# FFN input products of a two-layer diffusion step: two of the four weight sums of each block formed by transfers that add, on GpSimd's queue

## The chip, the cores and the metric

The kernel runs on one core of one Trainium2 chip. The metric is the device time of one execution in microseconds (us). The profile is one execution, recorded by the hardware profiler; instructions are put down to PE (TensorE's matmuls), PEld (its weight loads), DVE (VectorE), ACT (ScalarE), POOL (GpSimd) and SP (SyncE, which issues most transfers). A name with q behind it (SPq, POOLq) is an engine's instruction queue.

## The reference

One step of a trunk of two layers, over 512 latent and 128 context tokens (640 columns together), 1024 features, all in fp32. Each layer is an attention mixer and then a gated FFN with 2816 inner features; only the FFN matters here:

```python
def swiglu(h, w_in, w_out):
    gate, up = jnp.split(h @ w_in, 2, axis=-1)
    return (jax.nn.silu(gate) * up) @ w_out
...
        xp = xp + g2_p * swiglu(hp, w_ffn_in[l], w_ffn_out[l])
        xs = xs + g2_s * swiglu(hs, w_ffn_in[l], w_ffn_out[l])
```

## The kernel before

**Blocks.** The 2816 gate features and the 2816 up features are handled as 22 blocks of 128 (`FB` = 22). For block `fb` the weights are two tiles of 128 x 1024 fp32, `wg` (gate) and `wu` (up); columns 0 to 511 of each belong to the first 512 input features, the rest to the second 512. Every fp32 matmul is done as three: weights are split into a high part (a copy that rounds, on ACT) and a low part (the difference, on DVE), and so is the data.

**Seven products.** Blocks 0 and 1 are computed plainly (16 products of three matmuls per half of the columns). From block 2 (`FEW`) to block 21 a Strassen-Winograd scheme takes the 2 x 2 product of (gate, up) by (first, second inputs) with seven products of 12 matmuls, 320 columns each. It needs four weight operands: X is `wu` itself, W is the second half of `wg`, and Y and Z hold the four sums. With g0, g1 the halves of `wg` and u0, u1 those of `wu`: tile `s13` (Y) = [g0 + g1, u0 + g0], tile `s24` (Z) = [u0 + g0 + g1, u0 + g0 + g1 + u1]. `Weights.sums` forms the four sums on DVE, 512 columns each. `hi` and `lo` split X, Y and Z (1024 columns each), `hi_w` and `lo_w` split W (512 columns). In the profile's names, `s` stands for both `s13` and `s24`, and `wX`, `wY`, `wZ`, `wW` for the split operands.

**The loop.** `for fb in range(FEW, FB)` (L1468) issues PE's products of block `fb` and beside them prepares block `fb` + 1: `n.sums()`, then hi and lo of X, Y, Z and W. The result of block `fb` - 1 is finished there too: the gate's SiLU on ACT, the product `sg` on DVE, and its high and low parts `hd`, which SP stores to DRAM (`sp`). `step` brings the next layer's modulation weights `wm` (512 KB a block) and multiplies them on DVE into `junk`. `fetch_u` and `fetch_g` load the tiles `wu` and `wg` of block `fb` + 2 on SP's queue: `wu` into the pool `rawp` (3 buffers, shared with `wm`), `wg` into tag `wr` (2 buffers).

**The opening.** Before the loop, `ffn` computes blocks 0 and 1 and the first product of blocks 2 and 3 (`ahead`), while `ModS.make` and `add_up` form the seven data operands D, N, C, E and the two quarters of h (names `h01D`, `h01q` and so on in layer 0, `h11...` in layer 1). The unsplit data lies in spare tiles, `h0132a` (tag `cb`), `h0132d` (two, tag `wr`) and `h0132e` (tag `w4`); so the first `wg` tiles of the loop wait until `add_up` has read the `wr` tiles. The weights of block 1, `wgu_10` and `wgu_11`, come through two raw tiles of tag `ws`.

**Order.** Each engine runs its own list in order. The lists are made when the program is built: the framework's scheduler places instructions by the order of the code, by when it expects operands and buffers to be ready, and by `issue_after` hints; `Line` chains most of the loop's DVE work, and its ACT work, in the order in which it is written. A transfer waits on its queue until its buffer is free, and holds what is behind it in that queue.

Of the kernel before, what the change touches and what calls it, by code (L numbers as in the profile page):

```python
# [11 lines left out]
F32 = mybir.dt.float32  # L12
F32R = mybir.dt.float32r
AF = mybir.ActivationFunctionType
ALU = mybir.AluOpType
# [35 lines left out]
def body(ctx, tc, xT, vecs, crow, wm0, wm0g, wm1, wA, wNV, wNA, wMK, wMV, wOA, wGQ, wGK, wGV, wOC,  # L51
# [53 lines left out]
    def f(ap):  # L105
        return ap.bitcast(F32)
# [55 lines left out]
    def load(src, n, name):  # L162
        raw = rawp.tile([P, 1024], F32, tag="raw", name=name)
        nc.sync.dma_start(raw[:, :n], src)
        return raw[:, :n]
# [94 lines left out]
    class ModS:  # L260


        def __init__(self, name, x, gsl, ml, sh, pools):
            pool, keep_ = pools

            a = keep_.tile([P, 2 * D], F32, tag="cb", bufs=1, name=name + "32a")
            d = [pool.tile([P, 1024], F32, tag="wr", bufs=2, name=f"{name}32d{i}") for i in range(2)]
            d += [pool.tile([P, 1024], F32, tag="w4", bufs=2, name=f"{name}32e{i}") for i in range(2)]
            room = [t[:, j * HT:j * HT + HT] for t, n in zip([a] + d, (6, 3, 3, 3, 1)) for j in range(n)]
            self.left, self.right = room[:KT], room[KT:]  # L270
            self.name, self.x, self.gsl, self.ml, self.sh = name, x, gsl, ml, sh
            self.act = {}
            self.q = [[ring.tile([P, T], F32R, tag=("hh", "hl")[i], name=f"{name}q{k}{i}") for k in range(KT)] for i in range(2)]
            self.sums = {c: [pool.tile([P, T], F32R, tag="sums", bufs=16, name=f"{name}{c}{k}") for k in range(4)]
                         for c in "DCNE"}
# [927 lines left out]
    def ffn_open(l):  # L1203

        ph = ExitStack()
        fk = ph.enter_context(tc.tile_pool(name=f"fk{l}", bufs=1, reuse_waits="tile"))
        dr = ph.enter_context(tc.tile_pool(name=f"dr{l}", bufs=1, space=bass.MemoryType.DRAM))
        hd = [[fk.tile([P, T], F32R, name=f"hd{l}_{i}{c}") for c in "hl"] for i in range(1)]
        fs = ExitStack()
        fp = fs.enter_context(tc.tile_pool(name=f"fp{l}", bufs=1, reuse_waits="tile"))  # L1210
        w = []

        def pre():
            for i in range(2):
                w.append(unit(wFI[l, 0, i], 1024, f"wgu{l}_{i}", "vg"[i], pool=fp))
            w.append(unit(wFI[l, FEW, 1], 1024, f"wX{l}_{FEW}", pool=fp))
        return ph, fk, dr, hd, fs, fp, w, pre

    def scale_final(x, c, k):
# [3 lines left out]
    def ffn(l, x, pend, hm, nxt, side, opened):  # L1223
# [95 lines left out]

        def fetch_u(fb):  # L1320
            if fb < FB:
                raws[fb] = [load(wFI[l, fb, 1], 1024, f"wu{l}_{fb}r")]

        def fetch_g(fb):
            if fb == FEW:
                raws[fb].append(load(wFI[l, fb, 0], 1024, f"wg{l}_{fb}r"))
            elif fb < FB:
                rg = fp.tile([P, 1024], F32, tag="wr", bufs=2, name=f"wg{l}_{fb}r")
                nc.sync.dma_start(rg, wFI[l, fb, 0])
                raws[fb].append(rg)  # L1330

        class Weights:

            def __init__(self, fb):
                self.fb = fb
                self.u, self.g = raws[fb]
                self.X = wX[fb - FEW] if fb < FEW + AHEAD else None

            def sums(self):
                ru, rg = self.u, self.g  # L1340
                s13 = fp.tile([P, 1024], F32, tag="ws", bufs=2, name=f"s13{l}_{self.fb}")
                dve(V.tensor_tensor, s13[:, :512], rg[:, :512], rg[:, 512:], ALU.add)
                dve(V.tensor_tensor, s13[:, 512:], ru[:, :512], rg[:, :512], ALU.add)
                s24 = fp.tile([P, 1024], F32, tag="ws", bufs=2, name=f"s24{l}_{self.fb}")
                dve(V.tensor_tensor, s24[:, :512], s13[:, 512:], rg[:, 512:], ALU.add)
                dve(V.tensor_tensor, s24[:, 512:], s24[:, :512], ru[:, 512:], ALU.add)
                self.s = {"X": ru, "Y": s13, "Z": s24}
                self.t = {c: wtile(f"w{c}{l}_{self.fb}") for c in "XYZ" if c != "X" or self.X is None}
# [10 lines left out]
            def hi_w(self):  # L1359
                t = fp.tile([P, 2, 512], F32R, tag="w4", bufs=2, name=f"wW{l}_{self.fb}")  # L1360
                self.W = two(t)
                act(S.activation, self.W[0], self.g[:, 512:], AF.Copy)

            def lo_w(self):
                dve(V.tensor_tensor, self.W[1], self.g[:, 512:], f(self.W[0]), ALU.subtract)

        done = hm.done
        eight(0, w0, 0, range(3))
# [2 lines left out]
        wX = [w0[2]]  # L1371
        ahead(FEW, wX[0])
        wX += [unit(wFI[l, FEW + i, 1], 1024, f"wX{l}_{FEW + i}", behind=done) for i in range(1, AHEAD)]
        w1 = [unit(wFI[l, 1, i], 1024, f"wgu{l}_1{i}", behind=done, raw=fp.tile([P, 1024], F32, tag="ws", bufs=2, name=f"wgu{l}_1{i}r"))
              for i in range(2)]
        fetch_u(FEW)
        fetch_g(FEW)
# [90 lines left out]
        for fb in range(FEW, FB):  # L1468

            first = fb < FEW + AHEAD  # L1470
            n = Weights(fb + 1) if fb < FB - 1 else None
            b5 = bank(f"fd{l}_{fb}")
            up = tmp(f"up{l}_{fb}")
            sg = lead if paired and PAIR_OF.get(fb, (0, 1))[1] == 0 else tmp(f"sg{l}_{fb}")
            both = paired and job and job[0] in PAIR_OF
            p5, u1, g2 = [utile(f"{c}{l}_{fb}") for c in ("p5", "u1", "g2")]
            if n:
                n.sums()
            if n and not first:
                n.hi("X")  # L1480
            if fb in early:
                g = early[fb][0]
            else:
                g, b2, p1 = bank(f"fg{l}_{fb}"), bank(f"fu{l}_{fb}", "y"), utile(f"p1{l}_{fb}")
                product(g, w.X, 0, 11, True)
                act(S.activation, p1, g[:, :HT], AF.Copy)
            if n and not first:
                n.hi("Y")
                n.lo("X")
                n.hi("Z")  # L1490
                n.lo("Y")
                fetch_u(fb + 2)
            after(PE.last, lambda: product(b5, w.Y, 0, "D", True))
            act(S.activation, p5, b5[:, :HT], AF.Copy)
            if n and not first:
                n.lo("Z")
            if job:
                jb, jg, jW, jup, jsg = job
                product(jg, jW, 0, "E", False)
                if jb in early:  # L1500
                    dve(V.tensor_tensor, jsg[:, HT:T], jup[:, HT:T], jsg[:, HT:T], ALU.mult)
                act(S.activation, jsg[:, 0:HT], jg[:, :HT], AF.Silu, scale=-1.0)
                if jb in early:
                    dve(V.tensor_tensor, jsg[:, 0:HT], early[jb][1], jsg[:, 0:HT], ALU.mult)
                else:
                    dve(V.tensor_tensor, jsg, jup, jsg, ALU.mult)
            if n and not first:
                n.hi_w()
            if both:
                split_pair(jb, jsg, 0)  # L1510
            elif job:
                dh, dl = room(), room()
                act(S.activation, dh, jsg, AF.Copy)
            product(g, w.Z, 0, "N", False)
            act(S.activation, u1, g[:, :HT], AF.Copy)
            if n:
                if first:
                    for c in "XYZ":
                        n.hi(c)
                        n.lo(c)  # L1520
                    fetch_u(fb + 2)
                    n.hi_w()
                n.lo_w()
                fetch_g(fb + 2)
            if both:
                split_pair(jb, jsg, 1)
            elif job:
                dve(V.tensor_tensor, dl, jsg, f(dh), ALU.subtract)
                spill(jb, dh, dl)
            if fb not in early:  # L1530
                product(b2, w.X, 512, 21, True)
                dve(V.tensor_tensor, up[:, 0:HT], b2[:, :HT], p1, ALU.add)
            if both:
                split_pair(jb, jsg, 2)
            step("fb", fb, dve)
            step("load", fb + 1, act)
            product(b5, w.Z, 512, 22, False)
            dve(V.tensor_tensor, up[:, HT:T], b5[:, :HT], u1, ALU.add)
            product(g, w.Y, 512, "C", False)
            dve(V.tensor_tensor, g2, g[:, :HT], p5, ALU.add)  # L1540
            act(S.activation, sg[:, HT:T], g2, AF.Silu, scale=-1.0)
            job, w = (fb, g, w.W, up, sg), n
# [728 lines left out]
```

## Time and profile before

| | |
|---|---|
| times of three runs | 1481.51, 3368.07, 1478.6 us; median 1481.51 us |
| the profiled execution | 1480.2 us; its span 1478.4 us |
| PE busy | 1440.5 us, 97% of the span |
| DVE busy | 1202.6 us, 81% |
| ACT busy | 769.9 us, 52% |
| POOL busy | 210.9 us, 14% |
| FFN of layer 0, of layer 1 (input part) | about 377 to 650 us, about 1045 to 1318 us |

The span runs from the first to the last instruction of the profile; the rest of the execution's own time, 1.8 us, lies around it. A row of the timeline gives start, duration, engine, line, operation, output<-input, shapes and count; a duration includes the instruction's pipeline, so instructions that follow each other can start a little sooner than the one before has ended. A row of the table by stage gives, for each engine, the busy time and the number of instructions in that stage, then the clock granted to TensorE, the mean busy share of the 16 DMA engines, and GB/s.

### The profile page before, as it was taken

What the parts mean: (1) busy time and instruction counts of PE and PEld (TensorE: products, weight loads), DVE (VectorE), ACT (ScalarE), POOL (GpSimd) and SP (SyncE); (2) the same over time, 40 slices, a digit from 0 to 9 for tenths busy, and PEclk for the clock granted to TensorE, in tenths of its full rate; (3) what the DMA queues carried; (4) which work ended last, traced back from release to release, by engine and by line L of the source; (5) the groups of instructions that cost most, each with busy time, mean ns of one, the idle gap of its engine ahead of it and who ended that gap; (6) DMA issues with size and microseconds to landing.
All of it is one profiled execution on the core that took longest, in us unless ns stands there. A gap on an engine that the chain in (4) does not pass through costs nothing.

```text
span 1478.4 us, 25725 instructions
## 1 busy us (share of the span) xinstructions
PE 1440.5 (97%) x9785; PEld 1391.9 (94%) x9785; DVE 1202.6 (81%) x2236; ACT 769.9 (52%) x1521; POOL 210.9 (14%) x302
## 2 busy tenths in 40 slices
PE   5999999999999999999999999999999999999997
PEld 3988888889999999999999999989999999999996
DVE  5686688876989999967997888766999999954496
ACT  5446677863754544441123666663755555542253
POOL 0326534422000000000002322212000000000000
PEclk9999999999999999999999999999999999999998
DMA  9544521015065555569863210013055555668522
GB/s 372 219 152 142 178 67 37 29 55 189 30 204 190 189 184 182 168 229 336 271 217 114 95 55 31 29 44 123 29 196 169 190 197 209 207 224 303 196 86 72
DMA packets 80651, 229.53 MB, mean 155 GB/s; under 512 B 9136, under 2 KB 14736, under 8 KB 80144
## 3 DMA queue, kind: packets, MB, share of 16 engines
q1 hardware_dynamic: 77600, 220.51, 44.4%
q0 software_dynamic: 1728, 5.33, 1.0%
q10 hardware_dynamic: 1200, 2.05, 0.4%
q8 instruction: 77, 1.26, 0.3%
q14 instruction: 46, 0.38, 0.1%
HBM read 192.97 MB, written 34.89 MB: 154 GB/s over the span
## 4 chain that ended last, share of the span: by engine, by line
PE 85%; DVE 6%; ACT 4%; DMA 2%; issue 2%; SPq 0%; POOL 0%; DVEq 0%; ACTq 0%; POOLq 0%
PE fg L63 21%; PE fd L63 10%; PE fo L63 8%; PE fu L63 6%; PE gq L63 3%; DMA mraw<-in_wm 2%; PE nk L63 2%; PE nq L63 2%; PE fo_2b L63 1%; PE fo_0b L63 1%; PE gs L63 1%; PE fo_2a L63 1%; PE fo_0a L63 1%; PE go L63 1%; PE fo_4b L63 1%
## 5 line engine op out<-in xcount | busy, mean ns | idle before, releaser
L1805 DVE SCALAR_TENSOR_TENSOR junk<-wm,cb 128x1024 bf16<-128x1024 f32 x62 | 75.7, 1221 | 5.4 <-DMA wm<-in_wm 4.7
L1248 ACT ACTIVATE sg<-g 128x320 f32<-128x320 f32 x34 | 16.0, 472 | 115.0 <-DVE g L1248 115.0
L63 PE MATMUL gq<-h10h,wgq 128*128 128x320 f32 x256 | 66.7, 318 | 0.0
L255 POOL TENSOR_SCALAR h10h<-h10t,gs,mods 128x320 fp32r<-128x320 f32 x4 | 3.6, 888 | 429.5 <-DVE h10t L249 427.8
L1248 DVE SCALAR_TENSOR_TENSOR junk<-wm,cb 128x1024 bf16<-128x1024 f32 x50 | 61.1, 1221 | 0.8
L1248 DVE TENSOR_TENSOR wY<-s,wY 128x1024 fp32r<-128x1024 f32 x40 | 48.8, 1220 | 2.2 <-ACT wY L1248 2.2
L1248 DVE TENSOR_TENSOR wZ<-s,wZ 128x1024 fp32r<-128x1024 f32 x40 | 48.8, 1220 | 0.0
L63 PEld LDWEIGHTS gq<-h10h,wgq 128*128 128x128 f32 x256 | 45.0, 188 | 0.9 <-PE gtp L67 0.2
L1248 ACT ACTIVATE wZ<-s 128x1024 fp32r<-128x1024 f32 x40 | 42.4, 1060 | 0.1
L1248 ACT ACTIVATE wY<-s 128x1024 fp32r<-128x1024 f32 x40 | 42.0, 1049 | 0.0
L63 PE MATMUL gq<-h10l,wgq 128*128 128x320 f32 x128 | 39.5, 308 | 0.0
L1987 ACT ACTIVATE gp<-gs,gb,rq 128x640 f32<-128x640 f32 (+1 forms) x40 | 31.9, 797 | 14.5 <-DVE gb L1986 14.1
L63 PE MATMUL fg<-h11E,wW 128*128 128x320 f32 x240 | 38.7, 310 | 0.0
L63 PE MATMUL fg<-h11q,wX 128*128 128x320 f32 x240 | 38.6, 309 | 0.0
L63 PE MATMUL fg<-h01q,wX 128*128 128x320 f32 x240 | 38.6, 309 | 0.0
L63 PE MATMUL fg<-h11N,wZ 128*128 128x320 f32 x240 | 38.6, 309 | 0.0
L63 PE MATMUL fg<-h01N,wZ 128*128 128x320 f32 x240 | 38.6, 309 | 0.0
L63 PE MATMUL fu<-h01q,wX 128*128 128x320 f32 x240 | 38.6, 309 | 0.0
L63 PE MATMUL fu<-h11q,wX 128*128 128x320 f32 x240 | 38.6, 309 | 0.0
L63 PE MATMUL fg<-h01E,wW 128*128 128x320 f32 x240 | 38.6, 309 | 0.0
L63 PE MATMUL fd<-h11q,wZ 128*128 128x320 f32 x240 | 38.5, 309 | 0.0
L63 PE MATMUL fd<-h01q,wZ 128*128 128x320 f32 x240 | 38.5, 309 | 0.0
(3227 smaller groups left out, 5236.5 us busy)
## 6 DMA issues: line engine op xcount, KB each, us to landing
wm<-in_wm SPq DMA_DIRECT2D x48, 512.0 KB, 4.0
mraw<-in_wm SPq DMA_DIRECT2D x8, 1024.0 KB, 15.4
mraw<-in_wm SPq DMA_DIRECT2D x16, 512.0 KB, 3.9
hr_T<-sp_T SPq DMA_DIRECT2D x21, 320.0 KB, 5.8
hr_B<-sp_B SPq DMA_DIRECT2D x18, 320.0 KB, 6.2
mrow<-in_wm0g POOLq DMA_DIRECT2D x8, 512.0 KB, 6.4
wm<-in_wm0g SPq DMA_DIRECT2D x8, 512.0 KB, 3.5
x<-in_xT SPq DMA_DIRECT2D x8, 320.0 KB, 5.4
```

The costliest lines, as they stand in the source:

```text
L63: cls.last = nc.tensor.matmul(*a, **k)
L255: G.tensor_scalar(h[:, c0:c1], t, self.gsl[:, k, 0:1], self.ml[:, self.sh + k, 0:1], ALU.mult, ALU.add)
L1248: self.last = after(self.last, lambda: op(*a, **k))
L1805: def step(kind, at, line=lambda op, *a, **k: op(*a, **k)):
L1987: weighed.append((S.activation(dst, src, AF.Exp, bias=nb, scale=rq[:, j:j + 1], accum_out=ll[:, j:j + 1]), v))
```

## The change

The two sums of `s13` are no longer instructions of DVE. The tile `wg` grows to 1536 columns, and three transfers fill it for blocks 3 to 21 (block 2 stays as it was): SP writes g0 twice into columns 0 to 1023; once that has landed, a transfer on GpSimd's queue reads g1 and u0 from DRAM and adds them to these columns in place; SP writes g1 alone into columns 1024 to 1535. `fetch_g` now stands right behind `n.sums()`, earlier in the loop. To make room, `s24` has one buffer instead of two, the spare tiles of the opening are laid out differently, and the raw tiles of block 1's weights come from the tags `w4` and `ws`.

```diff
-            d = [pool.tile([P, 1024], F32, tag="wr", bufs=2, name=f"{name}32d{i}") for i in range(2)]
-            d += [pool.tile([P, 1024], F32, tag="w4", bufs=2, name=f"{name}32e{i}") for i in range(2)]
-            room = [t[:, j * HT:j * HT + HT] for t, n in zip([a] + d, (6, 3, 3, 3, 1)) for j in range(n)]
+            d = [pool.tile([P, 1536], F32, tag="wr", bufs=2, name=f"{name}32d{i}") for i in range(2)]
+            d.append(pool.tile([P, 1024], F32, tag="w4", bufs=2, name=f"{name}32e"))
+            room = [t[:, j * HT:j * HT + HT] for t, n in zip([a] + d, (6, 4, 4, 2)) for j in range(n)]
...
+            w.extend(fp.tile([P, 1024], F32, tag=tag, bufs=n, name=f"wgu{l}_1{i}r") for i, (tag, n) in enumerate((("w4", 2), ("ws", 1))))
...
-                rg = fp.tile([P, 1024], F32, tag="wr", bufs=2, name=f"wg{l}_{fb}r")
-                nc.sync.dma_start(rg, wFI[l, fb, 0])
-                raws[fb].append(rg)
+                t = fp.tile([P, 1536], F32, tag="wr", bufs=2, name=f"wg{l}_{fb}r")
+                g, y = wFI[l, fb, 0], t[:, :1024].rearrange("p (a b) -> p a b", a=2)
+
+                def from_(at, step):
+                    return bass.AP(tensor=g.tensor, offset=g.offset + at, ap=[list(g.ap)[0], [step, 2], [1, 512]])
+                nc.sync.dma_start(y, from_(0, 0))
+                nc.gpsimd.dma_start(y, from_(512, P * 1024 - 512), accum_op=ALU.add)
+                nc.sync.dma_start(t[:, 1024:], g[:, 512:])
+                raws[fb, 0] = t
...
-                s13 = fp.tile([P, 1024], F32, tag="ws", bufs=2, name=f"s13{l}_{self.fb}")
-                dve(V.tensor_tensor, s13[:, :512], rg[:, :512], rg[:, 512:], ALU.add)
-                dve(V.tensor_tensor, s13[:, 512:], ru[:, :512], rg[:, :512], ALU.add)
-                s24 = fp.tile([P, 1024], F32, tag="ws", bufs=2, name=f"s24{l}_{self.fb}")
-                dve(V.tensor_tensor, s24[:, :512], s13[:, 512:], rg[:, 512:], ALU.add)
+                ru, s13 = self.u, self.s13
+                if s13 is None:
+                    s13 = fp.tile([P, 1024], F32, tag="w4", bufs=2, name=f"s13{l}_{self.fb}")
+                    dve(V.tensor_tensor, s13[:, :512], self.g0, self.g, ALU.add)
+                    dve(V.tensor_tensor, s13[:, 512:], ru[:, :512], self.g0, ALU.add)
+                s24 = fp.tile([P, 1024], F32, tag="ws", bufs=1, name=f"s24{l}_{self.fb}")
+                dve(V.tensor_tensor, s24[:, :512], s13[:, 512:], self.g, ALU.add)
...
             if n:
                 n.sums()
+                fetch_g(fb + 2)
...
                 n.lo_w()
-                fetch_g(fb + 2)
```

How the built lists change. On DVE in the middle of the loop, from the sums of block 9 to its Z, before (wg_9r and wu_9r are the raw tiles):

```order
L1248 TENSOR_TENSOR s_9_6007<-wg_9r 128x512
L1248 TENSOR_TENSOR s_9_6007<-wu_9r,wg_9r 128x512
L1248 TENSOR_TENSOR s_9_6010<-s_9_6007,wg_9r 128x512
L1248 TENSOR_TENSOR s_9_6010<-s_9_6010,wu_9r 128x512
L1248 TENSOR_TENSOR wX_9_6013<-wu_9r,wX_9_6013 128x1024
L1248 TENSOR_TENSOR wY_9_6014<-s_9_6007,wY_9_6014 128x1024
L1248 TENSOR_TENSOR wZ_9_6015<-s_9_6010,wZ_9_6015 128x1024
```

and now:

```order
L1249 TENSOR_TENSOR s_9_6002<-wg_9r 128x512
L1249 TENSOR_TENSOR s_9_6002<-s_9_6002,wu_9r 128x512
L1249 TENSOR_TENSOR wX_9_6005<-wu_9r,wX_9_6005 128x1024
L1249 TENSOR_TENSOR wY_9_6006<-wg_9r,wY_9_6006 128x1024
L1249 TENSOR_TENSOR wZ_9_6007<-s_9_6002,wZ_9_6007 128x1024
```

Two sums are gone, the first remaining one reads the tile that the added transfer fills, and nothing else of the block has moved. On SP, the transfers of one block in the middle of the loop, before:

```order
L1329 DMA wg_10r<-in_wFI 128x1024
L1282 DMA sp_6h<-hd_0h 128x640
L1282 DMA sp_6l<-hd_0l 128x640
L164 DMA wu_10r<-in_wFI 128x1024
L164 DMA wm_44_6108<-in_wm0g 128x1024
```

and now; the third transfer of the tile stands behind the two stores, and the adding transfer is a row of POOL's list:

```order
L1334 DMA wg_10r<-in_wFI 128x2x512
L1283 DMA sp_6h<-hd_0h 128x640
L1283 DMA sp_6l<-hd_0l 128x640
L1336 DMA wg_10r<-in_wFI 128x512
L164 DMA wu_10r<-in_wFI 128x1024
L164 DMA wm_44_6102<-in_wm0g 128x1024
```

The first transfer of the tile stands where the one of before stood: both wait for `lo_w` of block 8, the last reader of the buffer. POOL's list, which held nothing in this part of the program, gets one row for each of the blocks 3 to 21, each writing the tile wg that SP's first transfer has filled:

```order
L1335 DMA wg_9r<-in_wFI 128x2x512
L1335 DMA wg_10r<-in_wFI 128x2x512
L1335 DMA wg_11r<-in_wFI 128x2x512
```

In the opening of the FFN (layer 0; layer 1 alike), the low parts of block 1's weights and the sums of block 2 (wg_2r, wu_2r) stood on DVE among the low parts of the data's right half (L298):

```order
L298 TENSOR_TENSOR h01q_4718<-h0132d_4706,h01q_4718 128x320
L185 TENSOR_TENSOR wgu_10_4988<-wgu_10r,wgu_10_4988 128x1024
L298 TENSOR_TENSOR h01q_4719<-h0132d_4706,h01q_4719 128x320
L185 TENSOR_TENSOR wgu_11_4993<-wgu_11r,wgu_11_4993 128x1024
L298 TENSOR_TENSOR h01q_4720<-h0132d_4706,h01q_4720 128x320
L298 TENSOR_TENSOR h01q_4721<-h0132e_4707,h01q_4721 128x320
L1248 TENSOR_TENSOR s_2_5003<-wg_2r 128x512
```

Now they stand behind all of those, and behind the gate of block 0 (`sg_0`) and part of `add_up` (L310 to L313):

```order
L1307 TENSOR_TENSOR sg_0_4999<-fu_00_4852,sg_0_4999 128x320
L312 TENSOR_TENSOR h0132a<-h0132a,h0132d_4707 128x320
L313 SCALAR_TENSOR_TENSOR h0132a<-h01n_5023,h0132a 128x320
L185 TENSOR_TENSOR wgu_10_4988<-wgu_10r,wgu_10_4988 128x1024
L185 TENSOR_TENSOR wgu_11_4992<-wgu_11r,wgu_11_4992 128x1024
L1249 TENSOR_TENSOR s_2_5002<-wg_2r 128x512
```

On ACT the two high parts moved likewise, from ahead of the right half's data to right behind the table load and the SiLU of block 0:

```order
L1306 ACT_TABLE_LOAD
L1306 ACTIVATE sg_0_4999<-fg_00_4851 128x320
L184 ACTIVATE wgu_10_4988<-wgu_10r 128x1024
L184 ACTIVATE wgu_11_4992<-wgu_11r 128x1024
```

They moved behind the table load, which is a wait that they did not stand behind before. Behind the sums of block 2, `add_up` and the gates follow on DVE as before, except that the second half of block 1's gate (`sg_1`) now stands ahead of the low part of block 2's Z (`wZ_2`). Outside the two FFN input parts the lists of all engines are the same.

More of the change, by code (lines that the diff above doesn't have):

```diff
@@ L1321, in fetch_u @@
             if fb < FB:
-                raws[fb] = [load(wFI[l, fb, 1], 1024, f"wu{l}_{fb}r")]
+                raws[fb, 1] = load(wFI[l, fb, 1], 1024, f"wu{l}_{fb}r")
         def fetch_g(fb):
             if fb == FEW:
-                raws[fb].append(load(wFI[l, fb, 0], 1024, f"wg{l}_{fb}r"))
+                raws[fb, 0] = load(wFI[l, fb, 0], 1024, f"wg{l}_{fb}r")
             elif fb < FB:
-                rg = fp.tile([P, 1024], F32, tag="wr", bufs=2, name=f"wg{l}_{fb}r")
-                nc.sync.dma_start(rg, wFI[l, fb, 0])
-                raws[fb].append(rg)
+                t = fp.tile([P, 1536], F32, tag="wr", bufs=2, name=f"wg{l}_{fb}r")
[6 more added lines that the diff above has]
+                raws[fb, 0] = t
         class Weights:
@@ L1335, in __init__ @@
                 self.fb = fb
-                self.u, self.g = raws[fb]
+                self.u, g = raws[fb, 1], raws[fb, 0]
+                self.g, self.s13 = (g[:, 512:], None) if fb == FEW else (g[:, 1024:], g[:, :1024])
+                self.g0 = g[:, :512]
                 self.X = wX[fb - FEW] if fb < FEW + AHEAD else None
             def sums(self):
-                ru, rg = self.u, self.g
-                s13 = fp.tile([P, 1024], F32, tag="ws", bufs=2, name=f"s13{l}_{self.fb}")
-                dve(V.tensor_tensor, s13[:, :512], rg[:, :512], rg[:, 512:], ALU.add)
-                dve(V.tensor_tensor, s13[:, 512:], ru[:, :512], rg[:, :512], ALU.add)
-                s24 = fp.tile([P, 1024], F32, tag="ws", bufs=2, name=f"s24{l}_{self.fb}")
-                dve(V.tensor_tensor, s24[:, :512], s13[:, 512:], rg[:, 512:], ALU.add)
+                ru, s13 = self.u, self.s13
[5 more added lines that the diff above has]
+                dve(V.tensor_tensor, s24[:, :512], s13[:, 512:], self.g, ALU.add)
                 dve(V.tensor_tensor, s24[:, 512:], s24[:, :512], ru[:, 512:], ALU.add)
@@ L1361, in hi_w @@
                 self.W = two(t)
-                act(S.activation, self.W[0], self.g[:, 512:], AF.Copy)
+                act(S.activation, self.W[0], self.g, AF.Copy)
             def lo_w(self):
-                dve(V.tensor_tensor, self.W[1], self.g[:, 512:], f(self.W[0]), ALU.subtract)
+                dve(V.tensor_tensor, self.W[1], self.g, f(self.W[0]), ALU.subtract)
         done = hm.done
@@ L1373, in ffn @@
         wX += [unit(wFI[l, FEW + i, 1], 1024, f"wX{l}_{FEW + i}", behind=done) for i in range(1, AHEAD)]
-        w1 = [unit(wFI[l, 1, i], 1024, f"wgu{l}_1{i}", behind=done, raw=fp.tile([P, 1024], F32, tag="ws", bufs=2, name=f"wgu{l}_1{i}r"))
+        w1 = [unit(wFI[l, 1, i], 1024, f"wgu{l}_1{i}", behind=done, raw=w0[3 + i])
               for i in range(2)]
```

## The prediction

> **What bounds the kernel now.** I read the page's shares first, then the table by stage for the two FFN input parts, then the waits of PE, then one block on the timeline. The page:
>
> ```profile
> span 1478.4 us, 25725 instructions
> PE 1440.5 (97%) x9785; PEld 1391.9 (94%) x9785; DVE 1202.6 (81%) x2236; ACT 769.9 (52%) x1521; POOL 210.9 (14%) x302
> GB/s 372 219 152 142 178 67 37 29 55 189 30 204 190 189 184 182 168 229 336 271 217 114 95 55 31 29 44 123 29 196 169 190 197 209 207 224 303 196 86 72
> ```
>
> PE is idle for 1478.4 - 1440.5 = 37.9 us in all. That is the most that any relief of another engine can win. Where does that idleness lie? The table by stage has both FFN input parts whole, and one stretch of three blocks in each:
>
> ```profile
> 395.00:650.00 255.00, 255.00 (x1740) 254.81 (x1740) 238.30 (x361) 130.69 (x222) 0.00 (x0) 1.00 0.55 178
> 1064.00:1318.00 254.00, 254.00 (x1733) 253.81 (x1733) 236.31 (x379) 139.04 (x251) 0.00 (x0) 1.00 0.57 188
> 444.00:481.00 37.00, 37.00 (x254) 37.00 (x254) 36.08 (x53) 18.77 (x32) 0.00 (x0) 1.00 0.60 189
> 1258.00:1295.00 37.00, 37.00 (x254) 37.00 (x254) 36.56 (x62) 21.13 (x39) 0.00 (x0) 1.00 0.63 206
> ```
>
> PE is busy for all of 255 and all of 254 us there, at a granted clock of 1.00, so none of the 37.9 us is in the parts that the change touches. The waits of PE say the same from the other side; the longest ones carry the names of a norm and of the final norm, and asked for those two stretches alone, the view has no entry:
>
> ```profile
> PE n00p L63 <- DVE n00acc L215: 7.9, 1, 7.9
> PE fn1p L63 <- DVE fn1acc L215: 1.8, 1, 1.8
> ```
>
> DVE, at 36.08 of 37 us, looks like a second bound, and it is not: it keeps step, and what it makes is ready ahead of PE. One block on the timeline:
>
> ```profile
> 470.45 1.22 DVE L1248 TENSOR_TENSOR wX<-wu_8r,wX 128x1024 fp32r<-128x1024 f32 x1
> ...
> 479.84 0.68 DVE L1248 TENSOR_TENSOR s<-wg_9r 128x512 f32<-128x512 f32 x1
> 480.44 0.69 DVE L1248 TENSOR_TENSOR s<-wu_9r,wg_9r 128x512 f32<-128x512 f32 x1
> 481.16 0.69 DVE L1248 TENSOR_TENSOR s<-s,wg_9r 128x512 f32<-128x512 f32 x1
> ...
> 486.64 0.69 DVE L1248 TENSOR_TENSOR wW<-wg_9r,wW 128x512 fp32r<-128x512 f32 x1
> ...
> 491.88 0.68 DVE L1248 TENSOR_TENSOR s<-wg_10r 128x512 f32<-128x512 f32 x1
> ```
>
> ```profile
> 478.44 1.92 PE L63 MATMUL fg<-h01q,wX 128*128 128x320 f32 x12
> ...
> 490.75 1.93 PE L63 MATMUL fg<-h01q,wX 128*128 128x320 f32 x12
> ```
>
> PE takes a block every 490.75 - 478.44 = 12.31 us, DVE's sums come every 491.88 - 479.84 = 12.04 us, and block 8's X is ready at 471.67, 6.8 us before PE starts on it at 478.44.
>
> **The change part by part.** *The sums that go.* Start to start, the two of block 9 take 0.60 + 0.72 = 1.32 us. Over blocks 3 to 21 of two layers, 38 blocks, DVE loses about 38 x 1.3 = 49 us of work. To the end this is worth nothing, because PE's 12.31 us a block cover all of DVE's 12.04; were that cover gone, up to 1.3 us a block would count. It buys slack: DVE needs about 10.7 of every 12.3 us.
>
> *The wait that is added, in the steady loop.* SP's first transfer stands where the old load stood and waits for the same reader, wW of two blocks before:
>
> ```profile
> 475.31 0.33 SPq L1329 DMA_DIRECT2D wg_10r<-in_wFI  x1
> ```
>
> The old load then had 491.88 - 475.31 = 16.6 us until its first reader. Now the first transfer (about 4.2 us, the row below), and behind it the adding one, A us from issue to landing, must both land. From a block's sums to the wW that frees its buffer DVE takes 486.64 + 0.69 - 479.84 = 7.5 us, less 1.3 for the two sums that go: 6.2 us. A buffer goes round in two blocks, 24.6 us, so the loop keeps PE's pace while 4.2 + A + 6.2 is below 24.6: A up to 14 us costs nothing. Behind DVE's waiting sum stand all the low parts of that block and its gate, behind ACT's waiting high part of Y those of Z and W; on POOL nothing but the next block's transfer, with POOL busy for 0.00 us in all four stages.
>
> No row shows an adding transfer, so A is bounded by the nearest ones: plain transfers, with queue, count, size and median time to landing, and for the one tile that POOL loads, its shortest, median and longest.
>
> ```profile
> wg_10r<-in_wFI SPq DMA_DIRECT2D x2, 512.0 KB, 4.2
> mraw<-in_wm SPq DMA_DIRECT2D x8, 1024.0 KB, 15.4
> mrow<-in_wm0g POOLq DMA_DIRECT2D x8, 512.0 KB, 6.4
> ...
> DMA to landing us min/median/max: 3.9/6.4/11.8
> wg_3r<-in_wFI SPq DMA_DIRECT2D x1, 512.0 KB, 3.4
> cb<-in_crow SPq DMA_DIRECT2D x1, 1024.0 KB, 5.0
> ```
>
> From below: 3.4 us, a plain load of this size with little beside it. From above: 15.4 us, a load that moves in bytes what this one reads twice over, in the busiest part of the program. My value: POOL's shortest, 3.9, plus the destination read as well, 512 KB at the rate of the stage above (189 GB/s at a share of 0.60 is 315 GB/s at full share, so 1.7 us), is 5.6; with other transfers beside it, A = 6. That is near POOL's own median of 6.4.
>
> The Trainium skill (DMA: Bandwidth & Descriptors, section Anatomy of one DMA — SWDGE (gpsimd) path) gives a fit for plain transfers from GpSimd of 2.0 us plus the bytes at 436 GB/s, an estimate of 3.2 us here. By it, without a second read, the sum below would lose its second term and be 1481.5; the shortest row on POOL, 3.9 us, is already longer than the fit.
>
> *The opening*, where the cover is thin. Layer 0; layer 1 repeats it 668.4 us later.
>
> ```profile
> 387.69 1.22 DVE L185 TENSOR_TENSOR wgu<-wgu_10r,wgu 128x1024 fp32r<-128x1024 f32 x1
> 389.23 1.22 DVE L185 TENSOR_TENSOR wgu<-wgu_11r,wgu 128x1024 fp32r<-128x1024 f32 x1
> ...
> 398.39 0.49 DVE L313 SCALAR_TENSOR_TENSOR h0132a<-h01n,h0132a 128x320 f32<-128x320 f32 x1
> ...
> 404.81 0.50 DVE L312 TENSOR_TENSOR h0132a<-h0132a,h0132d 128x320 f32<-128x320 f32 x1
> ...
> 409.63 1.23 DVE L1248 TENSOR_TENSOR wY<-s,wY 128x1024 fp32r<-128x1024 f32 x1
> ...
> 411.50 1.24 DVE L1248 TENSOR_TENSOR wZ<-s,wZ 128x1024 fp32r<-128x1024 f32 x1
> ```
>
> ```profile
> 394.13 1.28 ACT L1305 ACT_TABLE_LOAD   x1
> 395.42 0.44 ACT L1305 ACTIVATE sg<-fg 128x320 f32<-128x320 f32 x1
> ```
>
> ```profile
> 399.07 0.60 PE L63 MATMUL fg<-h01q,wgu 128*128 128x320 f32 x3
> ...
> 413.16 1.93 PE L63 MATMUL fd<-h01D,wY 128*128 128x320 f32 x12
> 414.92 1.92 PE L63 MATMUL fg<-h01N,wZ 128*128 128x320 f32 x12
> ...
> 420.20 1.93 PE L63 MATMUL fd<-h01D,wY 128*128 128x320 f32 x12
> ```
>
> ACT's high parts of wgu now stand behind that SiLU, from about 395.8 to 397.8, and DVE's low parts behind the gate that waits for the same SiLU (ends 395.86) and two rows of `add_up`: from about 397.2 to 399.5. Block 1 begins on PE at 399.07, and its third matmul, the first to need a low part, some 0.3 us later; the low part of the first tile is there at 398.4. That just fits. But what DVE did before the SiLU it now does after it, two low parts and four sums, 2 x 1.14 + 4 x 0.6 = 4.7 us, against 398.79 - 397.2 = 1.6 us by which it is there sooner. All of DVE behind is 3.1 us late. wY_2's low part ends at 410.86 + 3.1 = 414.0, against a D product that starts at 413.16 and needs it about 0.7 us in: level. wZ_2's, 0.4 further back behind `sg_1`, ends at 412.74 + 3.5 = 416.2, needed at about 415.6: PE loses 0.65 us, my first term.
>
> ```profile
> 405.38 0.33 SPq L1329 DMA_DIRECT2D wg_3r<-in_wFI  x1
> 407.75 0.33 SPq L1795 DMA_DIRECT2D cb<-in_crow  x1
> ```
>
> The first transfer for block 3 takes the buffer that held `h0132d`, and waits for its last read, the L312 row at 404.81, now at about 408. It is issued at 408.4 and lands at about 412.8, beside the 1 MB of `cb`; the adding one lands at 412.8 + A. From then DVE needs two sums (1.2), `hd_0l` (0.7) and wY_3's low part (1.2), and PE needs that at 420.20 + 0.65 + 0.3 = 421.1. So PE waits for max(0, A - 5) us: 1.0 at A = 6, my second term.
>
> *The sum.* 2 x (0.65 + 1.0) = 3.3 us on the profiled execution's 1480.2: **1483.5 us**. That execution and the median, 1481.51, differ by 0.1%. At A = 3.4 it is 1481.5; at 15.4 the opening takes 2 x (0.65 + 10.4) = 22 us and the loop (15.4 - 14)/2 a block, 0.7 x 36 = 25: 1527.
>
> **The rivals.** *No loss at all* (wY_2 and the waits of the opening fall into slack that I misjudged by a us): 1477 to 1481. For it speaks that PE's waits have no entry there; against it, that I count the lag row by row.
>
> *The transfers become the bound, slower than before.* 16 engines are busy for 0.60 x 12.31 = 7.4 us a block, 0.63 in layer 1, 7.8. The third transfer adds 256 KB, 0.8 us at the rate above; the adding one, read twice, 3.3 us. That makes 11.5 to 11.9 of 12.31 us: inside, but with little over, and if adding costs more engine time than a second read, past it. It decides from 12.31 - 7.8 - 0.8 = 3.7 us of all engines, 2.2 times a plain transfer's 1.7. At three times, 5.0 us, a block takes 7.6 + 0.8 + 5.0 = 13.4 us: 1.1 x 38 = 42 us and the opening, 1527; at four times 1590. Against it: a slice of the page reaches 372 GB/s, so the share counts waiting as well as moving, and the 189 GB/s of a block would rise to 189 + 64 = 253 for the 768 KB written more, 296 with the second read. Late transfers would show first in `wm`, issued only 4.9 us ahead of its reader (SP's row, then DVE's), where a load of this size takes about 4.2:
>
> ```profile
> 483.74 0.33 SPq L164 DMA_DIRECT2D wm<-in_wm0g  x1
> ...
> 488.67 1.21 DVE L1248 SCALAR_TENSOR_TENSOR junk<-wm,cb 128x1024 bf16<-128x1024 f32 x1
> ```
> The Trainium skill (DMA: Bandwidth & Descriptors, section Issuing engines are not separate DMA queues) says that transfers of all issuers interleave on the same 16 engines, so POOL's queue would bring no room of its own; the shares above count as if that held.
>
> *DVE was the bound after all.* Then 49 us go: 1431. Against it stands 255.00 of 255.00 us on PE.
>
> *The change doesn't do what it says*, sums or their waits not gone from DVE's path: about 1480, as before.
>
> **How the numbers follow.** Forecast (opening loses 1 to 10 us, the loop nothing) 0.60; no loss 0.17; transfers the bound, or A over 14, 0.18; DVE the bound 0.03; no change in what DVE does 0.02. 2% of the median, about what a measurement of this kernel can tell from no change, is 30 us: 1452 to 1511. Forecast, no loss and no effect lie within, 0.79; the slower rival starts at its edge, 0.18. The range takes in the upper end of A, which is also three times a plain transfer, and leaves out the DVE rival and about half of the slow one: 1476 to 1527.
>
> **What would show it.** DVE busy at about 1154 us, PE's waits still empty in both parts but for about 1.6 us at 415 to 421 and again 668 us later, the adding transfer landing in about 6 us, DMA share at 0.8 to 0.95. Wrong would be: a PE wait for wY, wZ or `s` in block after block, PE rows further apart than 12.31 us, or an adding transfer over 14 us.

## The result, and the profile after

The changed kernel takes 1501.53 us in the median (1498.57 to 1502.7), against 1480.1 us: a ratio of **1.0145, 95% interval 1.0122 to 1.0168**. That is inside the 2% that the prediction called no change and inside its range of 1476 to 1527, but the loss is 21 us where 3.3 were forecast. The ratio leaves out one run of the kernel before that took 3368.07 us. The page of the kernel after, to be read beside that of before; the last line is the share of all 16 engines that GpSimd's queue takes, which was 1.0%:

```profile
span 1499.9 us, 25844 instructions
...
PE 1449.1 (97%) x9785; PEld 1397.1 (93%) x9785; DVE 1164.0 (78%) x2160; ACT 769.7 (51%) x1521; POOL 257.2 (17%) x340
...
q0 software_dynamic: 12064, 25.26, 9.3%
```

DVE has 38.6 us less to do, and the span is 21.5 us longer. Three blocks of the loop in each layer, by the table of stages (busy times and counts of PE, PEld, DVE, ACT, POOL; granted clock; DMA share; GB/s):

```profile
444.00:481.00 37.00, 37.00 (x253) 36.82 (x252) 32.93 (x46) 22.78 (x37) 4.84 (x4) 1.00 0.91 262
1268.00:1305.00 37.00, 37.00 (x254) 37.00 (x254) 33.50 (x53) 19.73 (x37) 4.35 (x4) 1.00 0.91 263
```

In the loop nothing is lost: PE is busy for all of 37 us, although the transfer engines went from 0.60 to 0.91 (over all but the first blocks, 460 to 640 us, from 0.54 to 0.87). Two E products, one block apart, on the timeline of PE:

```profile
479.61 1.92 PE L63 MATMUL fg<-h01E,wW 128*128 128x320 f32 x12
...
491.92 1.92 PE L63 MATMUL fg<-h01E,wW 128*128 128x320 f32 x12
```

They stand 12.31 us apart, as before. So the loss is ahead of this. Block 2's E product, before and now:

```profile
422.11 2.03 PE L63 MATMUL fg<-h01E,wW 128*128 128x320 f32 x12
```

```profile
429.18 2.42 PE L63 MATMUL fg<-h01E,wW 128*128 128x320 f32 x12
```

It is 7.1 us late; block 3's is 9.5 us late, block 4's 10.0, and from there to the last block it stays at 10.0. Layer 1 adds the other 11.3 in the same place. The waits of PE, which had no entry in the two FFN input parts, now have these (first layer 0, then layer 1; us in all, times, longest):

```profile
PE fd L63 <- ACT wY L1249: 1.8, 1, 1.8
PE fd L63 <- DVE wY L1249: 1.7, 2, 1.5
PE fg L63 <- ACT u L1249: 1.7, 1, 1.7
...
PE fg L63 <- ACT u L1249: 4.0, 1, 4.0
PE fd L63 <- DVE wY L1249: 1.9, 2, 1.7
PE fd L63 <- ACT wY L1249: 1.2, 1, 1.2
```

Where they come from is one chain over five engines. SP's queue and POOL's at the opening of layer 0:

```profile
408.12 0.38 SPq L1334 DMA_DIRECT2D wg_3r<-in_wFI  x1
...
412.86 0.33 SPq L1283 DMA_DIRECT2D sp_0h<-hd_0h  x1
414.35 0.33 SPq L1283 DMA_DIRECT2D sp_0l<-hd_0l  x1
414.72 0.50 SPq L1334 DMA_DIRECT2D wg_4r<-in_wFI  x1
```

```profile
412.30 1.30 POOL L1335 DMA_DIRECT2D wg_3r<-in_wFI  x1 [37.65 <-DVE sg L1307]
423.61 1.22 POOL L1335 DMA_DIRECT2D wg_4r<-in_wFI  x1 [10.01 <-DMA wg_4r<-in_wFI]
```

and the transfers' sizes and median times to landing, two of the opening and two of the loop:

```profile
wg_3r<-in_wFI POOLq DMA_DIRECT2D x2, 512.0 KB, 9.3
wg_4r<-in_wFI SPq DMA_DIRECT2D x2, 512.0 KB, 8.2
wg_4r<-in_wFI POOLq DMA_DIRECT2D x2, 512.0 KB, 9.5
...
wg_10r<-in_wFI SPq DMA_DIRECT2D x2, 512.0 KB, 5.1
wg_10r<-in_wFI POOLq DMA_DIRECT2D x2, 512.0 KB, 6.8
```

Block 3's adding transfer lands 9.3 us after its issue, block 4's first transfer starts only at 414.72, behind two stores, and its two steps take 8.2 and 9.5 us. DVE, ACT and PE then show who stands behind the sums that wait for them (the bracket is the idle time before an instruction, and what ended it; "issue" names no releaser, and here the adding transfers of blocks 3 and 4 land at about 422 and 433):

```profile
422.20 0.69 DVE L1249 TENSOR_TENSOR s<-wg_3r 128x512 f32<-128x512 f32 x1 [5.75 <-issue]
...
433.00 0.69 DVE L1249 TENSOR_TENSOR s<-wg_4r 128x512 f32<-128x512 f32 x1 [4.96 <-issue]
...
434.33 0.48 DVE L1249 TENSOR_TENSOR sg<-up,sg 128x320 f32<-128x320 f32 x1
```

```profile
435.25 0.74 ACT L1249 ACTIVATE hd_2h<-sg 128x640 fp32r<-128x640 f32 x1 [3.17 <-DVE sg L1249]
435.89 0.42 ACT L1249 ACTIVATE u<-fg 128x320 f32<-128x320 f32 x1
```

```profile
413.64 1.73 PE L63 MATMUL fd<-h01D,wY 128*128 128x320 f32 x10 [0.19 <-DVE wY L1249]
...
425.55 3.03 PE L63 MATMUL fd<-h01D,wY 128*128 128x320 f32 x10 [1.54 <-DVE wY L1249]
...
436.37 2.03 PE L63 MATMUL fg<-h01C,wY 128*128 128x320 f32 x12 [1.69 <-ACT u L1249]
```

At 436.37 PE doesn't wait for block 4's weights at all. It waits for a copy `u` of block 3, which stands on ACT behind `hd_2h`, which needs the gate `sg` of block 2, which stands on DVE behind block 4's waiting sum. And ten matmuls of a D product that take 1.73 us at 413.64 take 3.03 at 425.55: PE is busy 8.6 us longer than before with the same number of matmuls, and rows like this are where it comes from: between 410 and 450 us 203 matmuls keep PE busy for 33.88 us, which at the rate of before (274 in 40.00) would take 29.6, and between 1085 and 1125 us 194 take 32.37 for 28.4, 8.2 us together. The other 12.9 of the 21.5 us are waits. The clock of the first of those stretches:

```profile
420.00:424.00 4.00, 2.20 (x12) 1.55 (x11) 1.76 (x3) 1.40 (x2) 0.39 (x1) 0.93 0.65 245
424.00:428.00 4.00, 2.46 (x10) 2.45 (x10) 4.00 (x6) 1.23 (x2) 0.83 (x1) 0.50 0.67 133
428.00:432.00 4.00, 4.00 (x22) 4.00 (x21) 0.03 (x1) 1.27 (x3) 0.00 (x0) 0.71 1.04 293
```

It was granted at 0.50 right after the first waits, and at 0.71 in the stretch after. The Trainium skill (TensorE: Matmul & The Clock Gate, section Part 1: The HAM clock gate) says that the array drops to half its rate after an idle window of about 3.4 us and comes back after a busy one of the same length; 0.50 agrees, though here no single wait of 3.4 us stood ahead of it, only waits of 1.80 and 1.54 us with two matmuls between.

### The profile page after: what moved, and what is told of

Read it like the earlier page. It is cut to its first block, busy times and chain, and to the rows that moved or that the text cites. A ratio compares the mean times of both kernels' runs of the same rounds, so it can differ in the third digit from the quotient of the medians.

```text
span 1499.9 us, 25844 instructions
## 1 busy us (share of the span) xinstructions
PE 1449.1 (97%) x9785; PEld 1397.1 (93%) x9785; DVE 1164.0 (78%) x2160; ACT 769.7 (51%) x1521; POOL 257.2 (17%) x340
## 4 chain that ended last, share of the span: by engine, by line
PE 75%; DVE 10%; ACT 6%; DMA 6%; issue 3%; SPq 0%; DVEq 0%; POOL 0%; ACTq 0%; POOLq 0%
PE fg L63 17%; PE fd L63 8%; PE fo L63 8%; PE fu L63 4%; PE gq L63 3%; PE nk L63 2%; DMA mraw<-in_wm 2%; PE fo_2b L63 1%; DMA wg_4r<-in_wFI 1%; PE gs L63 1%; PE nq L63 1%; PE fo_2a L63 1%; PE go L63 1%; PE fo_0b L63 1%; PE fo_0a L63 1%
## 5 line engine op out<-in xcount | busy, mean ns | idle before, releaser
L63 PE MATMUL fd<-h01D,wY 128*128 128x320 f32 x240 | 40.5, 317 | 3.5 <-ACT wY L1249 1.8
L63 PE MATMUL fd<-h11D,wY 128*128 128x320 f32 x240 | 40.3, 316 | 3.1 <-DVE wY L1249 1.9
L63 PE MATMUL fg<-h11C,wY 128*128 128x320 f32 x240 | 39.3, 313 | 4.0 <-ACT u L1249 4.0
L63 PEld LDWEIGHTS fd<-h01D,wY 128*128 128x128 f32 x240 | 37.2, 194 | 4.5 <-DVE wY L1249 2.4
L63 PEld LDWEIGHTS fd<-h11D,wY 128*128 128x128 f32 x240 | 37.1, 193 | 3.9 <-DVE wY L1249 2.5
L63 PEld LDWEIGHTS fg<-h11C,wY 128*128 128x128 f32 x240 | 36.7, 191 | 4.2 <-ACT u L1249 4.2
L63 PE MATMUL fg<-h01C,wY 128*128 128x320 f32 x240 | 38.7, 310 | 1.7 <-ACT u L1249 1.7
```

The source lines that it names most:

```text
L63: cls.last = nc.tensor.matmul(*a, **k)
```

## The experiments

Times are medians; each ratio is to the kernel before on the same chip, with its 95% interval.

**1. All sums back on DVE**, everything else as after: the layout and order of the opening, SP's larger transfers. The edit, with N = 99:

```diff
-                nc.gpsimd.dma_start(y, from_(512, P * 1024 - 512), accum_op=ALU.add)
+                if fb >= N:
+                    nc.gpsimd.dma_start(y, from_(512, P * 1024 - 512), accum_op=ALU.add)
...
+                elif self.fb < N:
+                    dve(V.tensor_tensor, s13[:, :512], s13[:, :512], self.g, ALU.add)
+                    dve(V.tensor_tensor, s13[:, 512:], s13[:, 512:], ru[:, :512], ALU.add)
```

> The kernel after, but without the adding transfers: SP's two transfers of the tile stay, and DVE forms the two sums of s13 in place, so the layout of the opening, its order on DVE and ACT and SP's list stay those of after. Theory (the loss is the adding transfer standing in the way of blocks 3 and 4 at the opening of each layer, the loop loses nothing): about 1 to 2.5 us over before, 1481 to 1483. Rival 1 (the opening's rearrangement, 3 us of DVE work later, is what costs): most of the 21 us stays, about 1495 to 1500. Rival 2 (the traffic of SP's larger transfers): a loss that stays in part, 1487 to 1495, with PE rows late in the loop.

Measured: 1485.24 us, 1.0034 (1.0022 to 1.0046). Three quarters of the loss are gone, so the adding transfers carry them. 0.34%, 5 us, stays without any of them, more than I gave the rearranged opening and the larger transfers together. The profiled execution, 2.8 us over the one before, shows where: its E products are 1.9 us late at the last block of layer 0 and 3.1 at the last of layer 1, and from block 5 of each layer on that lag doesn't grow. So in this execution all of it is lost at the openings, and SP's larger transfers cost nothing in the loop; what they cost at the opening itself the run doesn't show.

**2. Adding from block 5** (N = 5).

> The kernel after, with adding transfers for blocks 5 to 21 only; blocks 3 and 4 get their sums on DVE in place. Theory (opening alone): 1481 to 1483, the same as with all sums on DVE, although 34 of 38 adding transfers are there and the DMA share stays near 0.9. Rival (the adding transfers cost something in every block): 34/38 of the loss stays, about 1499.

Measured: 1484.51 us, 1.0032 (1.0021 to 1.0044), the same as with no adding transfer at all, with 34 of 38 of them in place. Its loop, as above:

```profile
444.00:481.00 37.00, 37.00 (x255) 37.00 (x254) 33.74 (x48) 18.91 (x32) 4.04 (x4) 1.00 0.95 275
```

The transfer engines are at 0.95 there, and PE is full. What adding does in the loop is hidden; the price is paid for blocks 3 and 4.

**3. Adding from block 4** (N = 4).

> The kernel after, with block 3's sums on DVE in place and adding transfers from block 4. Theory a (block 4 is late by itself: its first transfer is issued at about 415 us and the two transfers take 14 to 17 us, so its sums start at about 429 where PE's list wants them by about 424): a stall of about 5 us a layer stays, 1490 to 1494. Theory b (block 4 was late only because block 3 was): 1481 to 1484.

Measured: 1499.55 us, 1.0129 (1.0113 to 1.0144). Theory b is out, and theory a had the right place and was too low: block 4's adding alone costs 1.0129 - 1.0032 = 0.97%, 14 us, and block 3's on top of it only 1.0145 - 1.0129 = 0.16%, with intervals that overlap. No run has block 3's adding alone. PE's wait for `u` is longer than in the kernel after, since block 3 no longer delays what comes ahead of it:

```profile
433.73 3.45 PE L63 MATMUL fg<-h01C,wY 128*128 128x320 f32 x12 [4.52 <-ACT u L1249]
```

These twelve matmuls take 3.45 us instead of 1.92, the clock again (experiment 6).

**4. The gate ahead of the waiting sum.** As experiment 3, but block 2's gate and block 4's X stand ahead of block 4's sums on DVE and ACT:

```diff
-            if n:
+            if n and fb != FEW + 1:
                 n.sums()
                 fetch_g(fb + 2)
...
+            if fb == FEW + 1:
+                n.s, n.t = {"X": n.u}, {"X": wtile(f"wX{l}_{n.fb}")}
+                n.hi("X")
+                n.lo("X")
+                n.sums()
+                fetch_g(fb + 2)
```

> The kernel with adding transfers from block 4, but on DVE the gate of block 2 and X's low part of block 4 stand ahead of block 4's waiting sum, and on ACT X's high part stands ahead too. Theory (PE lost time there because the waiting sum held the gate, ACT's hd_2h behind the gate and the copy u_3 behind that, for which PE's C product of block 3 waits; block 4's own Y is wanted about 4 us later than u_3): most of the 14 us between this kernel's parent and the one with adding from block 5 goes, 1485 to 1490. Rival (the late Y of block 4 itself is the bound): 1496 to 1500 as the parent.

Measured: 1491.54 us, 1.0077 (1.0062 to 1.0092). Of the 0.97%, 0.52% are gone by order, with block 4's transfers as late as before in layer 0: `s` of block 4 starts at 430.83 here and at 430.36 in experiment 3. The time is 1.5 us over what I expected, and at least part of what stays has moved on by one block:

```profile
439.80 0.69 DVE L1249 TENSOR_TENSOR s<-wg_5r 128x512 f32<-128x512 f32 x1 [3.06 <-issue]
...
442.75 2.03 PE L63 MATMUL fd<-h01q,wZ 128*128 128x320 f32 x12 [1.57 <-ACT p L1249]
```

Now block 5's sum is the one that waits, and PE waits for a copy `p` behind it on ACT.

**5. `cb` later.** The kernel after, with the 1 MB load of `cb` issued behind block 4's transfers; that also put block 4's first transfer ahead of the store `sp_0h` (`side`, which issues the load, is called in the loop's first pass):

```diff
-            nc.sync.dma_start(cb, bass.AP(...))
+            after(hold[0], lambda: nc.sync.dma_start(cb, bass.AP(...)))   # hold[0]: block 4's third transfer
```

> The kernel after, but SP issues the 1 MB load of cb behind block 4's transfers, and block 4's first transfer ahead of the store sp_0h. Theory (block 4's chain is long since its first transfer waits in SP's queue until 414.7 us and then lands in 8.2 us beside cb, the stores and block 3's adding transfer): the first transfer is issued at 410 to 412, the adding one of block 3 lands in 7 to 8 us instead of 9.4, s_4 starts 3 to 5 us sooner, 1489 to 1495. Rival (landing at the opening is slow for another reason, the adding itself): 9.4 stays, 1497 to 1501.

Measured: 1491.23 us, 1.0076 (1.0061 to 1.0091), about half of the loss back.

```profile
wg_4r<-in_wFI SPq DMA_DIRECT2D x2, 512.0 KB, 3.6
wg_3r<-in_wFI POOLq DMA_DIRECT2D x2, 512.0 KB, 8.5
wg_4r<-in_wFI POOLq DMA_DIRECT2D x2, 512.0 KB, 12.4
```

Block 4's first transfer starts at 411.09 and lands in 3.6 us instead of 8.2, and `s` of block 4 comes at 427.64 instead of 433.00. Block 3's adding falls only to 8.5, more than I expected, and block 4's rises to 12.4: the two adding transfers now overlap. The 5.4 us that `s` comes sooner are about 3.6 of issue and 4.6 of the first landing, less 2.9 that the adding one takes longer. The edit moved `cb` and block 4's place in SP's queue together, so the run doesn't say which of the two shortened the first landing.

**6. PE kept busy through the wait.** As experiment 3, with three products more on PE ahead of the C product of block 3, whose result nothing reads:

```diff
+            if fb == FEW + 1:
+                idle = bank(f"idle{l}", "y")
+                for _ in range(3):
+                    after(PE.last, lambda: product(idle, w.X, 0, 11, True))
```

> The kernel with adding transfers from block 4, with three more products on PE (36 matmuls, 5.3 us at full clock, into a PSUM bank that nothing reads) right ahead of the C product of block 3, where PE waited 4.5 us in layer 0 and 7.0 in layer 1. Theory (part of the loss is that the granted clock falls behind such a wait, to 0.59 over 4 us in layer 0): the added work takes the place of the waiting, the clock stays at 1.00 there, C and X of block 3 and 4 run at full rate, and the whole is 1 to 4 us faster than its parent's 1499.6, 1495 to 1499. Rival (the fallen clock costs nothing, since the next waits absorb it): 1499 to 1501; if the added work itself stands in the way (more than the wait in layer 0 by 0.8 us): up to 1503.

Measured: 1495.62 us, 1.0095 (1.0079 to 1.0112): 0.34% faster than experiment 3 (1.0113 to 1.0144 there), by doing 10.6 us more work on PE. The intervals only just miss each other, the two were measured on different chips, and their profiled executions differ by 2.0 us, so the size is rough.

```profile
429.95 5.45 PE L63 MATMUL idle<-h01q,wX 128*128 128x320 f32 x36
435.24 1.92 PE L63 MATMUL fg<-h01C,wY 128*128 128x320 f32 x12
```

The C product behind it takes 1.92 us instead of 3.45. Against the rate of before, the matmuls between 410 and 450 and between 1085 and 1125 us take 5.4 us longer in experiment 3 and 1.8 here. The granted clock of the same stretch, in experiment 3 and here:

```profile
434.00:438.00 4.00, 4.00 (x18) 4.00 (x18) 3.35 (x3) 3.04 (x4) 0.00 (x0) 0.59 1.06 242
```

```profile
434.00:438.00 4.00, 4.00 (x29) 4.00 (x28) 2.57 (x3) 3.81 (x6) 0.00 (x0) 1.00 0.89 161
```

**7. A transfer that copies, not adds**, on the same queue (Y and Z are other numbers).

> The kernel after, but POOL's transfer copies over the tile and doesn't add (so Y and Z are other numbers). If adding costs one more read of 512 KB (1.7 us of all engines): it lands in about 5.7 us in the loop instead of 7.4, 7 to 8 at the opening instead of 9.4, queue 0 takes about half of its 9.3% share, and the time is 1492 to 1497. If adding costs nothing over copying: 7.4 and 9.4 us, and 1500 as before.

Measured: 1493.44 us (one run). What GpSimd's queue takes, and how block 3's and 4's transfers land:

```profile
q0 software_dynamic: 7200, 25.26, 5.0%
...
wg_3r<-in_wFI POOLq DMA_DIRECT2D x2, 512.0 KB, 6.3
wg_4r<-in_wFI POOLq DMA_DIRECT2D x2, 512.0 KB, 7.8
```

Less the 14.8 us of before (1.0% of 1478.4), adding takes 9.3% of 1499.9 - 14.8 = 124.7 us of all engines for 38 transfers, **3.28 us each**; copying takes 5.0% of 1491.7 - 14.8 = 59.8 us, **1.57 each**. Adding costs 2.1 times a copy. In the loop (medians over blocks 6 to 21) it lands in 7.4 us, a copy in 5.6, and POOL's own instruction takes 1.20 us against 0.72.

**8. DVE's relief alone:** the kernel before with `s13 = rg` for its two sums, so Y is split from the raw tile.

> The kernel before without the two sums of s13 and with nothing in their place (Y is split from the raw tile, so its numbers are others), in all 40 blocks: what DVE's relief alone is worth. Theory (PE bounds the loop): DVE busy falls by about 50 us, the time by nothing, 1478 to 1481. Rival (DVE bounds): 1430 to 1440.

Measured: 1481.35 us, 1.001 (1.0 to 1.0019).

```profile
PE 1441.0 (97%) x9785; PEld 1391.9 (94%) x9785; DVE 1162.2 (78%) x2156; ACT 768.9 (52%) x1521; POOL 210.2 (14%) x302
```

DVE does 40.4 us less, and nothing comes of it. Even for free, taking these sums off DVE gains nothing in this kernel.

**9. Adding twice from block 5** (Y is other numbers): is there room in the loop?

> The kernel with adding transfers from block 5, each issued twice in a row (so Y is other numbers): does the loop have room left? The engines' share is 0.9 in the loop with one; a second one adds 3.3 us of all engines a block, 27%, and 7.4 us to the chain. If the engines' share is a bound: a block takes 1.17 x 12.3 = 14.4 us, 34 x 2.1 = 71 us more, 1555. If only the chain counts (first landing 4.5 + 2 x 7.4 + 6.2 = 25.5 against 24.6 us for two blocks): 0.5 us a block, about 1500.

Measured: 1588.08 us (one run), over both expectations: 104 us over experiment 2, 3.1 a block. Neither theory holds as I put it.

```profile
460.00:640.00 180.00, 159.93 (x1016) 156.37 (x1015) 129.47 (x185) 73.27 (x123) 28.97 (x24) 0.94 0.92 240
```

The engines are at 0.92 over these 180 us (0.91 in layer 1), against 0.83 with one adding transfer. Four stretches of 37 us lie between 0.87 and 0.95 here and between 0.86 and 0.95 there, so the share doesn't tell the two kernels apart. The chain can be followed from block 11's first transfer to block 13's, which takes the same buffer:

```profile
509.25 0.38 SPq L1334 DMA_DIRECT2D wg_11r<-in_wFI  x1
...
539.34 0.38 SPq L1334 DMA_DIRECT2D wg_13r<-in_wFI  x1
```

```profile
516.55 1.20 POOL L1336 DMA_DIRECT2D wg_11r<-in_wFI  x1 [8.99 <-DMA wg_11r<-in_wFI]
525.20 1.20 POOL L1338 DMA_DIRECT2D wg_11r<-in_wFI  x1 [7.44 <-DMA wg_11r<-in_wFI]
```

```profile
533.15 0.69 DVE L1249 TENSOR_TENSOR s<-wg_11r 128x512 f32<-128x512 f32 x1 [6.88 <-DMA wg_11r<-in_wFI]
```

The first transfer takes 7.3 us until POOL goes on, the two adding ones 8.7 and 7.9, and from the sums to wW and block 13's transfer it is 6.2: 30.1 us for two blocks, each step released by the one before, for PE's 24.6. That is 2.7 us a block, most of the 3.1. So in this stretch the chain is the bound, with each landing longer than I put in; how much of that is crowding on the engines no run parts. The clock of 0.94 goes with PE's waits behind it: waits of 2.59 and 0.74 us stand ahead of two groups that take 3.07 and 3.57 us instead of 1.92 (from 505.95 on).

## Why the prediction was right, and where it was not

- **The range held by luck.** The forecast that got most weight was a loss of 1 to 10 us at the opening, and 21 lies outside it. The range took the time in because its upper end was worked out for A = 15.4, with 22 us lost at the opening and 25 in the loop. Measured are an A of 9.3 at the opening, no loss in the loop, and a loss at block 4 that the sum didn't have.
- **No gain from DVE's relief**: right, by experiment 8. Its size was read too high, 49 us for 38.6; it changed nothing.
- **No loss in the loop up to A of 14 us**: right. A is 7.4 us in the loop where I took 6, and PE keeps its 12.31 us. The engines' share came out at 0.87 to 0.91, where 11.5 to 11.9 of 12.31 us would be 0.93 to 0.97, and an adding transfer takes the 3.3 us that I gave it, read twice. The rival of transfers that become the bound didn't come.
- **The issue of block 3's first transfer**: predicted 408.4, landing at 412.8; measured 408.12, and POOL issues behind it at 412.30.
- **The second term was mis-sized**: A at the opening is 9.3 us, not 6. By the prediction's own formula, A - 5, that is 4.3 us a layer for 1.0. The formula comes near: at block 2's E product the kernel after is 4.5 us (layer 0) and 3.9 us (layer 1) further behind than that of experiment 1. The value was POOL's shortest row, 3.9, and 1.7 for the second read. At this place a plain copy already takes 6.3 (experiment 7) and adding 3.0 more, so the busy place, at a share of 0.98 from 412 to 420 us beside `cb` and two stores, was the larger part of the miss.
- **A term was missing, and it is the largest**: block 4. The prediction took one waiting sum for the opening and went over to the steady state, where a first transfer is issued 16.6 us ahead of its reader. Block 4's is issued at 414.72, and before, its sum ran at 421.98, 7 us for two transfers:

  ```profile
  421.98 0.68 DVE L1248 TENSOR_TENSOR s<-wg_4r 128x512 f32<-128x512 f32 x1
  ```

  Both rows could have been had: SP's queue with the stores ahead of it, and DVE's list. Experiment 3 puts it at 0.97%, 14 us.
- **Who stands behind the waiting sum** was named for the loop ("its gate") and not followed at the opening, where it decides. Experiment 4 takes back half of block 4's loss by order, with the transfers about as late.
- **A wait on PE costs more than its length.** The prediction counted waits as lost time, one for one. 8.6 of the 21.5 us are matmuls that ran slower behind waits. By experiment 6 the fallen clock behind waits of 4.5 and 7.0 us was worth about 5 us of block 4's 14 by the ratios, 2 by the two profiles.
- **The first term, 0.65 us a layer for the opening's order**, was too small: experiment 1 gives 5 us for both layers by the ratio and 3.1 by its profiled execution, at the openings alone. PE's named waits there, 0.2 us for block 2's wY and 0.5 for a copy `p`, are near the term, though the prediction had it waiting for wZ. Where the rest is lost stays open.

By the runs the 21 us are: about 5 without any adding, 14 for block 4's, about 2 for block 3's once block 4's is there, none for blocks 5 to 21.

## What to carry to other kernels

Before work is moved to transfers, ask whether the engine that is relieved has anyone waiting for it; here the stage's table said no, and a run with the work simply left out confirmed it. A longer chain that the steady state hides is paid for where the pipeline fills: work through the first two or three rounds one by one, with the place of each transfer in its queue, and not only the first. A waiting instruction should stand behind everything in its engine's list that others need first, since in-order engines pass a wait on; the version with adding from block 5 keeps most of DVE's relief (1169.4 us busy for 1202.6) at 1.0032, but none beats the kernel before.

## What the runs showed of the hardware

- An adding transfer of 512 KB on GpSimd's queue occupies the 16 engines for 3.28 us, 2.1 times a copy of the same shape (1.57), and lands in 7.4 us beside a loop's other traffic, 5.6 for the copy; two that overlap at the opening take 8.5 and 12.4 (experiment 5).
- The transfer engines' share reached 0.95 over 37 us of the loop without holding up PE, and was 0.92 over 180 us in the kernel with twice the adding, which was 7% slower and bound by a chain of transfers: the share alone doesn't tell when transfers are in the way.
- After waits of 4.5 to 7 us the granted clock stood at 0.50 to 0.59 for about 4 us, and so it did in the kernel after behind two waits of 1.80 and 1.54 us with two matmuls between them. Behind one wait of 1.67 us (experiment 5, layer 0) ten matmuls took 1.73 us, the full rate. 36 useless matmuls a layer in the longer wait made the kernel 0.34% faster.
